# A hybrid decoder layer in fp32: both gate/up and down products of its FFNs in seven block products

## The chip, the cores and the metric

The kernel runs on one core of one Trainium2 chip. The metric is device time in microseconds (us), from the start to the end of one execution; a time given for a kernel is the median of several runs. The core's engines work side by side and wait for each other through semaphores: TensorE (PE in the profile, its weight loads PEld), VectorE (DVE), ScalarE (ACT), GpSimd (POOL) and SyncE (SP). SyncE, ScalarE and GpSimd also start DMA transfers, each on a queue of its own.

## What is computed

The layer has 256 tokens of 2048 channels. Two feed-forward networks (FFNs) with 5632 inner channels stand around a mixer of two attention branches; each of the three steps ends in a LayerNorm.

```
def _swiglu(x, w_gate, w_up, w_down):
    return (jax.nn.silu(x @ w_gate) * (x @ w_up)) @ w_down
...
        h = _layer_norm(ALPHA * h + 0.5 * _swiglu(h, ffn1_w_gate[l], ffn1_w_up[l], ffn1_w_down[l]),
                        ln1_g[l], ln1_b[l])
        mix = _mixer(h, positions, w_in[l], mla_q_norm_g[l], mla_w_uq[l], mla_kv_norm_g[l],
...
        h = _layer_norm(ALPHA * h + mix, ln2_g[l], ln2_b[l])
        h = _layer_norm(ALPHA * h + 0.5 * _swiglu(h, ffn2_w_gate[l], ffn2_w_up[l], ffn2_w_down[l]),
                        ln3_g[l], ln3_b[l])
```

Everything is fp32. The change is in the two FFNs and in how they begin.

## The kernel before

**Products.** TensorE multiplies a 128x128 piece of the activations (held as its stationary operand) by a 128x512 piece of the weights. To keep fp32's accuracy every operand is first split in two: ScalarE rounds it to a short form, `hi` (line 149), and VectorE subtracts that from the original, which gives `lo` (line 150). A product is then three matmuls, hi·hi, hi·lo and lo·hi (`triple`, lines 201 to 204). The tokens stand in two blocks of 128, so a weight piece is used twice, once for each block.

**Weights.** A unit is one DMA of 512 KB: two 128x512 pieces side by side, so 1024 columns. It comes on SyncE's queue into one of four `raw` buffers (or into an `sraw` buffer, see below) and is split into a pair of tiles of the ring `wring`. One unit with both token blocks is worth 12 matmuls. `unit` and `advance` hold a look-ahead: loads are issued some units before the split, and splits some units before the matmuls; `lag` keeps the products of the second token block some units behind those of the first. Buffers bound how early a load can start. Within each engine the build then fixes one order of instructions, and the engine executes in that order: an instruction that waits holds up all behind it.

**Gate/up in seven products.** The 5632 inner channels are worked in 11 pairs of column chunks; a chunk has 256 gate and 256 up columns. The 2048 input channels are four quads of 512, each 2 units of weights. The first pair is computed plainly, with 16 units of 12 matmuls (`project`, called in `ffn`). The pairs 1 to 10 (`Hybrid.group`) treat quads 0 and 1 as a 2x2 block product: quads 0 and 1 of x for the two token blocks against blocks 11, 21 (chunk w0) and 22 (chunk w1) of the weights. Seven block products take the place of eight: products 1 to 7, in two halves of six matmuls each, with sums of x on the one side (the forms `xs`, made once per FFN in `Seven`: sums, differences and a negative, each split) and sums of weight blocks on the other. The sums of weights are made in the buffers themselves: after block 11 has been split for product 1, a DMA from GpSimd adds the corresponding block of w1 to it in place (line 325), and it is split again for product 5; VectorE then joins block 22 to it (line 320), it is split again for 6, and so on. Quads 2 and 3 of x stay plain. Products land in PSUM banks named X, Y, Z, W; ScalarE copies bank X out after products 1, 6 and 7 and Z after 5 (`snap`), and `sum_done` joins bank and copy on VectorE.

**From gate/up to down.** h = silu(gate)·up (lines 503 and 507) is turned on VectorE (line 495) and written to DRAM as `hT` by GpSimd (line 497). `get_h` reads it back by quads (line 525), and `split_h` splits it. Before the down projection the program drains its look-ahead (`look(0, 0)`, `catch_up(0)`, `flush()`). Down takes 11 quads of h against four column chunks, one after the other, 22 units of 12 matmuls each, all plain; h is split in the first chunk and kept for the other three. Each chunk ends in the eviction of two banks into z with its statistics (lines 450 to 454), and after the fourth the LayerNorm is applied block by block (`apply`, lines 459 to 486), transposed by TensorE (line 382) and split for the next stage.

**The beginning.** x is loaded in pieces of 128x512 on ScalarE's queue (line 912, `load_x`) and split as it comes. TensorE runs 32 short matmuls on zeros meanwhile (line 98).

## Time and profile before

| what | value |
| --- | --- |
| median of 3 runs | 2049.41 us (2049.03 to 2052.78) |
| the profiled execution | 2047.69 us, its span from the first to the last instruction 2045.9 us |
| mean granted TensorE clock | 0.996 of full speed |
| DMA | 453.14 MB in all, 221 GB/s over the span |
| joins of gate/up (line 507) | the first at 35.3 us, the last of FFN2 at 1796.4 |
| evictions of down (line 452) | the first at 536.3, the last at 2035.2 us |
| evictions of the mixer into LayerNorm 2 (line 450) | 1268.3 to 1338.6 us |

The span is told in us from its first instruction. FFN1's gate/up goes to about 470 us, its down projection to about 710, the mixer to about 1340, and FFN2 from there to the end. PE, DVE and so on are busy times; a row of the timeline has start, duration, engine, line, operation, output<-inputs, and in square brackets how long the engine had been idle before it and what it waited for.

### The profile page before, as it was taken

To read this page: it belongs to the slowest core of one execution; us is meant where nothing else is said; L and a number is where in the kernel's file an instruction comes from. 1 tells how busy PE (TensorE), PEld (TensorE's weight loads), DVE (VectorE), ACT (ScalarE), POOL (GpSimd) and SP (SyncE) were. 2 spreads that over 40 slices of the span, in tenths; PEclk is the share of its full clock that TensorE was granted. 3 is DMA by queue.
4 is the path that set the end of the run, shared out by engine and by line. 5 is a ranking of instruction groups with operands and counts; after the bars stand their busy time and mean duration, and the time that the engine had idled before them with its cause. 6 is when DMAs were issued, how large, how long until landed. Compare 5 with 4: busy or idle time off the path is not lost.

```text
span 2045.9 us, 25157 instructions
## 1 busy us (share of the span) xinstructions
PE 2019.2 (99%) x9088; PEld 1669.7 (82%) x9088; DVE 1429.5 (70%) x1685; ACT 1146.3 (56%) x1443; POOL 219.9 (11%) x359
## 2 busy tenths in 40 slices
PE   8999999999999999999999999999999999999997
PEld 7788888887888888888888888878888888878886
DVE  6788888887555575455665555688888888865545
ACT  5666666666433565554674445476666666753332
POOL 1112111222000000000000000011211121220000
PEclk9999999999999999999999999999999999999999
DMA  7877887898655756544545575667788788986553
GB/s 274 244 224 225 269 261 224 227 281 318 203 194 194 242 174 202 171 154 153 171 164 187 191 275 187 213 230 233 226 271 258 220 231 271 293 284 195 196 192 138
DMA packets 129437, 453.14 MB, mean 221 GB/s; under 512 B 17104, under 2 KB 17184, under 8 KB 129312
## 3 DMA queue, kind: packets, MB, share of 16 engines
q1 hardware_dynamic: 102240, 366.52, 51.9%
q0 software_dynamic: 25920, 82.91, 17.7%
q10 hardware_dynamic: 1152, 2.10, 0.3%
q8 instruction: 71, 1.16, 0.2%
q14 instruction: 54, 0.44, 0.1%
HBM read 433.64 MB, written 17.83 MB: 221 GB/s over the span
## 4 chain that ended last, share of the span: by engine, by line
PE 87%; DMA 4%; issue 4%; DVE 3%; ACT 1%; POOL 1%; DVEq 0%; ACTq 0%; POOLq 0%; SPq 0%
PE mm L203 28%; PE mm L202 28%; PE mm L204 28%; DVE wring L150 1%; DMA sraw<-in_gu_dram 1%; DMA xraw<-in_xT_dram 1%; DMA hraw<-hT 1%; DMA z<-in_x_dram 1%; ACT wring L149 0%; POOL hT L497 0%; DMA row_i<-in_pos_row_dram 0%; PE tr L382 0%; PE tr L664 0%; DVE h L150 0%; DMA raw<-in_gu_dram 0%
## 5 line engine op out<-in xcount | busy, mean ns | idle before, releaser
L150 DVE TENSOR_TENSOR wring<-raw,wring 128x1024 fp32r<-128x1024 f32 (+1 forms) x582 | 701.9, 1210 | 463.6 <-ACT wring L149 460.2
L149 ACT CAST wring<-raw 128x1024 fp32r<-128x1024 f32 (+1 forms) x582 | 605.0, 1042 | 566.3 <-PE mm L204 507.3
L202 PE MATMUL mm<-wring,h 128*128 128x512 f32 (+2 forms) x1632 | 635.0, 389 | 1.8 <-ACT h L149 1.8
L204 PE MATMUL mm<-wring,h 128*128 128x512 f32 (+2 forms) x1632 | 630.1, 387 | 0.6 <-DVE h L150 0.6
L203 PE MATMUL mm<-wring,h 128*128 128x512 f32 (+2 forms) x1632 | 629.4, 386 | 0.4 <-DVE wring L150 0.4
L149 ACT CAST wring<-sraw 128x1024 fp32r<-128x1024 f32 x280 | 292.6, 1053 | 179.5 <-PE mm L204 74.7
L150 DVE TENSOR_TENSOR wring<-sraw,wring 128x1024 fp32r<-128x1024 f32 x280 | 336.3, 1217 | 51.1 <-ACT wring L149 46.4
L202 PEld LDWEIGHTS mm<-wring,h 128*128 128x128 f32 x1632 | 306.7, 188 | 63.6 <-ACT h L149 3.6
L204 PEld LDWEIGHTS mm<-wring,h 128*128 128x128 f32 x1632 | 306.5, 188 | 63.3 <-DVE h L150 2.2
L203 PEld LDWEIGHTS mm<-wring,h 128*128 128x128 f32 x1632 | 306.7, 188 | 61.5 <-DVE wring L150 1.5
L203 PE MATMUL mm<-wring,xs 128*128 128x512 f32 x560 | 218.8, 391 | 3.9 <-DVE wring L150 3.9
L202 PE MATMUL mm<-wring,xs 128*128 128x512 f32 x560 | 218.4, 390 | 1.6 <-ACT snap L305 1.6
L204 PE MATMUL mm<-wring,xs 128*128 128x512 f32 x560 | 218.4, 390 | 0.0
L202 PE MATMUL mm<-wring,x 128*128 128x512 f32 x384 | 150.6, 394 | 5.7 <-ACT x L149 4.5
L203 PE MATMUL mm<-wring,x 128*128 128x512 f32 x384 | 150.5, 393 | 0.4 <-DVE wring L150 0.4
L204 PE MATMUL mm<-wring,x 128*128 128x512 f32 x384 | 150.0, 392 | 0.0
L203 PEld LDWEIGHTS mm<-wring,xs 128*128 128x128 f32 x560 | 105.4, 188 | 26.7 <-DVE wring L150 5.2
L202 PEld LDWEIGHTS mm<-wring,xs 128*128 128x128 f32 x560 | 105.3, 188 | 24.4 <-ACT snap L305 2.5
L204 PEld LDWEIGHTS mm<-wring,xs 128*128 128x128 f32 x560 | 105.4, 188 | 21.8
L497 POOL DMA_DIRECT2D hT<-blocks x176 | 97.1, 560 | 208.6 <-DVE blocks L495 205.2
L325 POOL DMA_DIRECT2D sraw<-in_gu_dram x80 | 70.4, 880 | 440.5 <-DVE wring L150 380.9
L320 DVE TENSOR_TENSOR sraw<-sraw,sraw 128x1024 f32<-128x1024 f32 x80 | 95.9, 1219 | 0.5
(240 smaller groups left out, 1616.1 us busy)
## 6 DMA issues: line engine op xcount, KB each, us to landing
raw<-in_gu_dram SPq DMA_DIRECT2D x192, 512.0 KB, 5.5
raw<-in_dn_dram SPq DMA_DIRECT2D x176, 512.0 KB, 4.2
sraw<-in_gu_dram SPq DMA_DIRECT2D x120, 512.0 KB, 6.5
sraw<-in_gu_dram POOLq DMA_DIRECT2D x80, 512.0 KB, 8.3
raw<-in_wgm_dram SPq DMA_DIRECT2D x32, 512.0 KB, 3.4
raw<-in_wgd_dram SPq DMA_DIRECT2D x32, 512.0 KB, 3.4
raw<-in_w_out_dram SPq DMA_DIRECT2D x32, 512.0 KB, 3.8
hT<-blocks POOLq DMA_DIRECT2D x176, 64.0 KB, 2.7
```

Of the source, the lines that this page charges most:

```text
L149: S.copy(hi, src)
L150: V.tensor_tensor(out=lo, in0=src, in1=hi.bitcast(F32), op=ALU.subtract)
L202: PE.matmul(o, xh, wh, start=first, stop=False, skip_group_check=again)
L203: PE.matmul(o, xh, wl, start=False, stop=False, skip_group_check=again)
L204: PE.matmul(o, xl, wh, start=False, stop=last, skip_group_check=again)
L320: V.tensor_tensor(out=t, in0=t, in1=R[joins[p]][s], op=ALU.add)
L325: nc.gpsimd.dma_start(R[adds[p]][s], w1[s], accum_op=ALU.add)
L497: nc.gpsimd.dma_start(hT[q, b].rearrange("(g r) (i f) -> i r g f", g=4, i=4)[i], t[32 * i:32 * (i + 1), :].rearrange("r (g f) -> r g f", g=4))
```

## The change

It has four parts.

1. *The first pair of gate/up is in seven products too* (`group` with `opening=True`). Its plain units, quads 2 and 3 of x, come first and the seven products between and behind them; each result has a bank of its own. The forms of x are made by `sevens`, attached to units 5 to 13. PSUM is one pool of eight banks instead of five and three.
2. *x comes on SyncE's queue*, between the weights: quads 2 and 3 first, then 0 and 1, which are not split by themselves any more (only their forms are). LayerNorm 2 hands over in the order 2, 3, 0, 1, for the same reason.
3. *Down is done in two passes of two column chunks each* (`c0`, `c1`). In each pass four of the eleven quads of h (two blocks of two) are in seven products, whose forms are made anew in each pass; seven quads are plain. h is fetched and split in both passes (`get`, `put`, `take`); nothing of it is kept. Product sums are gathered by `gather` into z.
4. *The joints.* Gate/up and down are one list of units; down begins with quads 4 and 5 in its first pass, with 4 in its second, and the look-ahead runs on from the one to the other.

The diff, cut to its core:

```diff
@@ -83,10 +83,10 @@
         return small.tile([P, n], dt, tag="sm", name=nm(name), bufs=24)
 
     def mm_bank(name="mm"):
-        return psum.tile([P, 512], F32, tag="mm", name=nm(name), bufs=5)
+        return psum.tile([P, 512], F32, tag="bank", name=nm(name), bufs=8)
 
     def tr_bank(name="tr"):
-        return psum.tile([P, 512], F32, tag="tr", name=nm(name), bufs=3)
+        return mm_bank(name)
...
+        def sevens(self, d, blocks=False):
+            ra, rc = self.raw(2 * d), self.raw(2 * d + 1)
+            at = self.forms.setdefault(d, {})
+            st = {}
...
+            def sums():
+                a0, a1, c0, c1 = (of_raw(r, b) for r in (ra, rc) for b in range(2))
...
+                for out, in0, in1 in ((f5, a1, c1), (f7, a1, a0), (f6, a0, f5), (f3, c0, f6)):
+                    V.tensor_tensor(out=out, in0=in0, in1=in1, op=ALU.subtract)
...
+            return [minus, lambda: pair(None, 2, 4), sums, lambda: pair(st["a"], 5, 6), lambda: pair(st["b"], 7, 3)]
...
+        def seven(self, d, p, then=None):
+            fresh = {1: ("A", 0, 0), 2: ("E", 0, 2), 3: ("D", 1, 2)}
+            src = {1: "A", 5: "A", 6: "A", 4: "A", 2: "E", 3: "D", 7: "D"}[p]
+            joins = {6: "D", 4: "E"}
+            adds = {1: "A", 6: "D"}
...
+                    t = self.blocks[src, s]
                     if p in joins:
-                        V.tensor_tensor(out=t, in0=t, in1=R[joins[p]][s], op=ALU.add)
+                        V.tensor_tensor(out=t, in0=t, in1=self.blocks[joins[p], s], op=ALU.add)
                     pair = next_pair()
                     split(*pair, t)
                     st["pair"] = [v.rearrange("p (g n) -> p g n", g=G) for v in pair]
                     if p in adds:
-                        nc.gpsimd.dma_start(R[adds[p]][s], w1[s], accum_op=ALU.add)
+                        nc.gpsimd.dma_start(self.blocks[adds[p], s], self.w[1][4 * d + s], accum_op=ALU.add)
...
-            rest = list(range(j0, end))
-            for p, n in ((1, 0), (2, 1), (5, 1), (3, 0), (6, 1), (4, 1), (7, 0)):
...
+        if opening:
+            seq = [(0, 4), (0, 5), (1, 4), (1, 5), (0, 6), 1, (1, 6), 2, (0, 7), 5, (1, 7), 3, 6, 4, 7]
+        else:
+            seq = [1, 2, (0, 4), 5, (0, 5), 3, 6, (0, 6), 4, (0, 7), 7, (1, 4), (1, 5), (1, 6), (1, 7)]
...
-            for c in range(4):
+            for c in (2, 3, 0, 1) if self.x.kept else range(4):
...
-        project(wgu[0], x, KD, 512, lambda b, bank: gu_done(0, b, bank), hook=first_hook)
-        project(wgu[1], x, KD, 512, lambda b, bank: gu_done(1, b, bank), hook=second)
-        look(3, 4)
...
-                later(13, lambda: split_h(0))
...
-        for c in range(4):
-            project(wdn[c], h, KF, 512, lambda b, bank, c=c: ln.evac(c, b, bank), hook=more if c == 0 else dn_hook(c))
...
+        for p in range(KF // 4):
+            items += group(x, wgu[2 * p], wgu[2 * p + 1],
+                           lambda n_, b, bank, snap, op, p=p: sum_done(2 * p + n_, b, bank, snap, op), p == 0)
+        for i, f in zip((5, 7, 10, 11, 13), x.sevens(0)):
+            at(i, f)
+        if first is not None:
+            first(at)
+        at(12, lambda: narrow(), True)
...
+        def get(i, q):
+            nc.gpsimd.dma_start(hx[i].raw(q), hT[q].rearrange("b p f -> p b f"))
...
+        for i, (c0, c1) in enumerate(((0, 1), (2, 3))):
+            pr = Pair(hx[i], wdn[c0], wdn[c1], "stream")
...
+            def seven(d, q, last, i=i, pr=pr, gather=gather):
+                t = len(items)
+                at(t - 16, lambda: get(i, 2 * d))
+                at(t - 14, lambda: get(i, 2 * d + 1))
+                for k, f in enumerate(hx_forms(i, d)):
+                    at(t - 7 + k, f)
+                at(t - 2, lambda: get(i, q))
+                for b in range(2):
+                    at(t + b, lambda b=b: put(i, q, b))
+                pl = [pr.plain(n, 2 * q + g) for n in range(2) for g in range(2)]
+                r = []
+                for p in (1, 2, None, 5, None, 3, 6, None, 4, None, 7):
...
+            if i == 0:
+                at(len(items), lambda: st.update(ln=LayerNorm(0.5, residual, g, bt, each, nxt, cols)), True)
+                for q in (4, 5):
+                    items += lone(q)
+            else:
+                items += lone(4)
+            items += seven(0, 6 if i == 0 else 5, False)
+            items += lone(7 if i == 0 else 6)
+            items += seven(1, 8 if i == 0 else 7, True)
+            if i == 0:
+                for q in (9, 10):
+                    items += lone(q)
+            else:
+                at(len(items) - 8, lambda: st["ln"].take_rows(), True)
+                at(len(items), widen, True)
+                for n in range(2):
+                    for q in (8, 9, 10):
+                        items += lone(q, (n, n), True)
...
     def load_x(q, b):
-        raw = xq.raw(q, b) if q in xq.kept else tmp_tile([P, 512], "xraw")
-        nc.scalar.dma_start(raw, a["xT"][q, b])
-        xq.put(q, b, raw.rearrange("p (k t) -> p k t", k=4))
-
-    def start_hook(j):
-        if j in (2, 4, 6):
-            load_x(j // 2, 0)
-        if 1 <= j < 5:
-            load_x(j - 1, 1)
+        nc.sync.dma_start(xq.raw(q)[:, b, :], a["xT"][q, b])
+        if q > 1:
+            xq.put(q, b, xq.raw(q)[:, b, :].rearrange("p (k t) -> p k t", k=4))
+
+    def first(at):
+        for i, q, b in ((0, 2, 0), (1, 2, 1), (4, 3, 0), (4, 3, 1), (5, 0, 0), (5, 0, 1), (5, 1, 0), (5, 1, 1)):
+            at(i, lambda q=q, b=b: load_x(q, b), True)
```

What this does to the order of the instructions shows at three places. The first is VectorE in FFN1's opening (`raw`, `sraw`: weights as loaded; `wring`: their lo part; `xs`: forms of x). Before, the first block product's weights `sraw_77` are split in the second pair and split again, after the added block, eight rows later:

```order
L150 TENSOR_TENSOR wring_22_125<-sraw_77_451,wring_21_124 128x1024
L150 TENSOR_TENSOR wring_20_123<-sraw_78_452,wring_19_122 128x1024
L150 TENSOR_TENSOR wring_18_121<-sraw_79_453,wring_17_120 128x1024
L150 TENSOR_TENSOR wring_16_119<-sraw_80_454,wring_15_118 128x1024
L507 TENSOR_TENSOR hb_48_285<-mm_55_297,sg_75_442 128x256
L150 TENSOR_TENSOR wring_6_109<-raw_87_468,wring_5_108 128x1024
L150 TENSOR_TENSOR wring_22_125<-sraw_78_452,wring_21_124 128x1024
L507 TENSOR_TENSOR hb_57_312<-mm_63_334,sg_90_494 128x256
L495 STREAM_TRANSPOSE blocks_92_497<-hb_48_285 128x512
L150 TENSOR_TENSOR wring_4_107<-sraw_77_451,wring_3_106 128x1024
```

After, the block is `sraw_40` and stands in the first pair:

```order
L190 TENSOR_TENSOR wring_22_125<-raw_52_306,wring_21_124 128x1024
L190 TENSOR_TENSOR wring_12_115<-sraw_40_229,wring_11_114 128x1024
L190 TENSOR_TENSOR xs_41_234<-neg_42_235,xs_41_234 128x512
L190 TENSOR_TENSOR wring_10_113<-sraw_44_252,wring_9_112 128x1024
L190 TENSOR_TENSOR wring_20_123<-sraw_40_229,wring_19_122 128x1024
L190 TENSOR_TENSOR wring_8_111<-raw_47_266,wring_7_110 128x1024
L190 TENSOR_TENSOR xs_49_271<-xraw_24_128,xs_48_270 128x1024
L190 TENSOR_TENSOR wring_10_113<-sraw_44_252,wring_9_112 128x1024
L190 TENSOR_TENSOR wring_8_111<-raw_58_341,wring_7_110 128x1024
```

The first split has moved forward among the first units, and two rows stand between it and the second.

The second place is TensorE at the end of LayerNorm 2, where FFN2 opens (`h2`: the layer's normalized activations; `tr`: transposes of z; `mm`: banks). Before:

```order
L202 MATMUL mm_1338_9884<-wring_530_4955,h2_1329_9856 128x512
L203 MATMUL mm_1338_9884<-wring_531_4956,h2_1329_9856 128x512
L382 MATMUL tr_1350_9978<-ident_70,z_1251_9273 128x128 x4
L382 MATMUL tr_1353_9992<-ident_70,z_1251_9273 128x128 x4
L382 MATMUL tr_1354_10004<-ident_70,z_1252_9274 128x128 x4
L204 MATMUL mm_1338_9884<-wring_530_4955,h2_1330_9857 128x512
L202 MATMUL mm_1338_9884<-wring_530_4955,h2_1329_9856 128x512
L203 MATMUL mm_1338_9884<-wring_531_4956,h2_1329_9856 128x512
L382 MATMUL tr_1358_10019<-ident_70,z_1252_9274 128x128 x4
L204 MATMUL mm_1338_9884<-wring_530_4955,h2_1330_9857 128x512
L202 MATMUL mm_1365_10041<-wring_524_4949,h2_1351_9987 128x512
```

After:

```order
L246 MATMUL mm_1453_10149<-wring_7_110,h2_1440_10080 128x512
L247 MATMUL mm_1453_10149<-wring_8_111,h2_1440_10080 128x512
L248 MATMUL mm_1453_10149<-wring_7_110,h2_1440_10080 128x512
L430 MATMUL tr_1463_10211<-ident_70,z_1366_9512 128x128 x4
L430 MATMUL tr_1466_10225<-ident_70,z_1366_9512 128x128 x4
L430 MATMUL tr_1469_10239<-ident_70,z_1365_9511 128x128 x4
L430 MATMUL tr_1470_10249<-ident_70,z_1365_9511 128x128 x4
L246 MATMUL mm_1453_10149<-wring_7_110,h2_1440_10080 128x512
L247 MATMUL mm_1453_10149<-wring_8_111,h2_1440_10080 128x512
L248 MATMUL mm_1453_10149<-wring_7_110,h2_1440_10080 128x512
L246 MATMUL mm_1478_10268<-wring_1410_9929,xs_1476_10263 128x512
```

Behind the transposes of the second token block came plain products with `h2`, of this block in a bank of its own; now a block product comes, whose stationary operand is a form `xs`.

The third is VectorE in the down projection. Before, it held splits of weights (`raw`) and evictions into z with their statistics (`bn`):

```order
L150 TENSOR_TENSOR wring_22_125<-raw_481_4359,wring_21_124 128x1024
L150 TENSOR_TENSOR wring_20_123<-raw_483_4378,wring_19_122 128x1024
L452 SCALAR_TENSOR_TENSOR z_379_3535<-mm_458_4005,z_379_3535 128x512
L454 BN_STATS bn_393_3551<-z_379_3535 128x6
L150 TENSOR_TENSOR wring_18_121<-raw_485_4395,wring_17_120 128x1024
L452 SCALAR_TENSOR_TENSOR z_381_3537<-mm_460_4030,z_381_3537 128x512
L454 BN_STATS bn_394_3552<-z_381_3537 128x6
```

After, forms of h (`fa`, `fb`, `xs`), h itself and block A of the weights (`sraw_460`) stand between:

```order
L190 TENSOR_TENSOR wring_22_125<-sraw_460_3666,wring_21_124 128x1024
L168 TENSOR_TENSOR fb_471_3719<-hraw_437_3524,fa_470_3718 128x512
L190 TENSOR_TENSOR xs_474_3742<-fa_470_3718,xs_473_3741 128x1024
L190 TENSOR_TENSOR wring_20_123<-sraw_464_3690,wring_19_122 128x1024
L190 TENSOR_TENSOR xs_477_3763<-fb_471_3719,xs_476_3762 128x1024
L190 TENSOR_TENSOR wring_10_113<-sraw_469_3714,wring_9_112 128x1024
L190 TENSOR_TENSOR wring_8_111<-sraw_472_3736,wring_7_110 128x1024
L190 TENSOR_TENSOR h_480_3812<-hraw_478_3780,h_480_3812 128x512
L190 TENSOR_TENSOR h_483_3826<-hraw_478_3780,h_483_3826 128x512
L190 TENSOR_TENSOR wring_6_109<-raw_475_3757,wring_5_108 128x1024
L190 TENSOR_TENSOR wring_4_107<-sraw_460_3666,wring_3_106 128x1024
L323 TENSOR_TENSOR sraw_460_3666<-sraw_460_3666,sraw_482_3822 128x1024
```

Block A's first split is the first row, its second, after the added block, the last but one; nine rows lie between.

More of the change, by code (lines that the diff above doesn't have):

```diff
@@ L190, in unit @@
             load()
-        loaded.append((prep, now, later_on))
+        todo_now = [*doing, now]
+        doing.clear()
+        loaded.append((prep, lambda: [f() for f in todo_now], later_on))
         advance(*ahead)
@@ L368, in group, with plain @@
[L368 to L377 removed]
+            return [lambda s=s: one(s) for s in range(2)]
+        def plain(self, n, j, then=None, apart=False):
+            return [lambda: self.plain_unit(n, j, then, apart)]
@@ new lines, in plain_unit, with load, prep, products @@
+        def plain_unit(self, n, j, then, apart):
+            st = {}
+            def load():
+                st["raw"] = wpool.tile([P, 1024], F32, tag="raw", name=nm("raw"), bufs=4)
+                nc.sync.dma_start(st["raw"], self.w[n][j])
+            def prep():
+                pair = next_pair()
+                split(*pair, st["raw"])
+                st["pair"] = [v.rearrange("p (g n) -> p g n", g=G) for v in pair]
+            def products(b):
+                wh, wl = st["pair"]
+                o, first = self.bank((n, b))
+                for g in range(G):
+                    k = 2 * j + g
+                    triple(o, self.x.at(0, k, b), self.x.at(1, k, b), wh[:, g, :], wl[:, g, :],
+                           first and g == 0, g == 1, True)
+                if then is not None:
+                    then(b)
+            if apart:
+                unit(load, prep, lambda: products(0), lambda: products(1))
+            else:
+                unit(load, prep, lambda: (products(0), products(1)))
@@ L574, in at_unit @@
+        for i, item in enumerate(items):
+            for f in before.get(i, ()):
+                f()
+            doing.extend(attached.get(i, ()))
+            item()
     def at_unit(u, fn):
```

361 lines of the change are left out of this document (195 added, 166 removed).

## The prediction

> **What bounds the kernel now.** I read the summary of the page first, then the busy time of the engines in stretches that follow the stages, then the groups of instructions.
>
> ```profile
> span 2045.9 us, 25157 instructions
> PE 2019.2 (99%) x9088; PEld 1669.7 (82%) x9088; DVE 1429.5 (70%) x1685; ACT 1146.3 (56%) x1443; POOL 219.9 (11%) x359
> ```
>
> TensorE is busy for 99% of the span, so the time is the number of matmuls times their pitch, plus a few stalls. The table by stretches (columns: length, then busy time and count of PE, PEld, DVE, ACT, POOL; granted clock, DMA share, GB/s) shows where they are.
>
> ```profile
> 0.00:50.00 50.00, 44.10 (x186) 36.39 (x187) 33.11 (x39) 28.54 (x36) 5.49 (x16) 0.93 0.78 271
> 50.00:100.00 50.00, 45.16 (x189) 36.06 (x188) 38.94 (x60) 29.94 (x37) 9.90 (x16) 0.97 0.85 247
> 100.00:430.00 330.00, 330.00 (x1457) 273.29 (x1457) 286.94 (x301) 210.41 (x245) 64.33 (x97) 1.00 0.83 244
> 430.00:520.00 90.00, 87.44 (x382) 70.97 (x381) 69.41 (x79) 58.25 (x74) 26.72 (x48) 1.00 0.87 289
> 520.00:710.00 190.00, 190.00 (x840) 157.39 (x839) 97.84 (x87) 77.84 (x74) 0.54 (x1) 1.00 0.63 204
> 1330.00:1400.00 70.00, 69.18 (x315) 55.51 (x315) 60.93 (x86) 48.19 (x79) 12.35 (x20) 1.00 0.67 214
> 1790.00:1860.00 70.00, 68.53 (x301) 55.69 (x300) 46.72 (x53) 35.85 (x45) 14.06 (x26) 1.00 0.76 261
> 2020.00:2046.00 26.00, 15.12 (x67) 12.20 (x65) 15.02 (x32) 0.41 (x2) 0.00 (x0) 0.89 0.22 81
> ```
>
> From 100 to 430 us (gate/up in seven products) 330 us hold 1457 matmuls, 0.2265 us each, with no gap; VectorE is busy for 87% of it. In the down projection (520 to 710) VectorE has only 51%. The first 100 us hold 375 matmuls, 32 of them short warming ones; the other 343 are worth 77.7 us, so TensorE is 22.3 us late by then. The joints from gate/up to down lose 2.6 and 1.5 us.
>
> What the splits cost is in the groups (mean ns after the comma):
>
> ```profile
> L150 DVE TENSOR_TENSOR wring<-raw,wring 128x1024 fp32r<-128x1024 f32 (+1 forms) x582 | 701.9, 1210 | 463.6 <-ACT wring L149 460.2
> L149 ACT CAST wring<-raw 128x1024 fp32r<-128x1024 f32 (+1 forms) x582 | 605.0, 1042 | 566.3 <-PE mm L204 507.3
> L320 DVE TENSOR_TENSOR sraw<-sraw,sraw 128x1024 f32<-128x1024 f32 x80 | 95.9, 1219 | 0.5
> L612 DVE SCALAR_TENSOR_TENSOR bias<-dist,mask 128x384 f32<-128x384 f32 x4 | 2.0, 551 | 0.0
> L630 DVE SCALAR_TENSOR_TENSOR ang<-turns,ang 128x128 f32<-128x128 f32 x12 | 3.4, 280 | 0.0
> ```
>
> Back to back they overlap a little, as the timeline shows:
>
> ```profile
> 5.51 0.69 DVE L150 TENSOR_TENSOR x<-xraw,x 128x512 fp32r<-128x512 f32 x1 [4.51 <-ACT x L149]
> 18.08 1.90 DVE L150 TENSOR_TENSOR x<-xraw,x 128x512 fp32r<-128x512 f32 x3 [0.35 <-ACT x L149]
> 22.24 4.73 DVE L150 TENSOR_TENSOR wring<-raw,wring 128x1024 fp32r<-128x1024 f32 x4
> 435.16 0.43 DVE L507 TENSOR_TENSOR hb<-gus,sg 128x256 f32<-128x256 f32 x1 [0.61 <-ACT sg L503]
> ```
>
> Four of 1024 columns take 4.73 us, a pitch of 1.17; three of 512 take 1.90, a pitch of 0.61; one of 256 costs some 0.36.
>
> **The change, part by part.**
>
> *Fewer matmuls: -27.2 us.* An opening pair of gate/up goes from 16 x 12 = 192 products to 7 x 12 + 8 x 12 = 180. A down pass (two of the four column chunks) goes from 44 x 12 = 528 to 504, as each of its two blocks saves 12. Per FFN that is 12 + 48 = 60, in all 120 x 0.2265 = 27.2. The Trainium skill (TensorE: Matmul & The Clock Gate, "Wait - 56ns, not 53.3ns?") gives 215.7 ns for a warm pitch of 512 columns; by it this term would be 25.9 us, but here 1457 matmuls show 226.5 ns, and the row decides.
>
> *The joints: -4.0 (0 to -4.1).* Before, everything is drained and h is then fetched and split. After, down begins with quads 4 and 5, written several groups earlier, and leaves 9 and 10 to the end. The 2.6 + 1.5 us go; next late is VectorE.
>
> *Down on VectorE: +4 (0 to +22).* Per FFN the change makes of 88 splits 112, and adds 16 joins, a second splitting of h and the forms of its four blocks: 128 x 1.17 = 149.8; 28 pieces of h x 0.61 = 17.1; forms 4 x (7 x 0.61 + 2 x 1.17) = 26.4; bank sums, joins into z, evictions and statistics 32 x 0.61 = 19.5; the tail of the last gate/up group 5.1. That is 218 us against 1008 x 0.2265 = 228.3: VectorE goes from 51% to 95%, with 10 us to spare. Into that falls a wait: block A is split, w1 is added to it by a DMA from GpSimd, and it is split again.
>
> ```profile
> L325 POOL DMA_DIRECT2D sraw<-in_gu_dram x80 | 70.4, 880 | 440.5 <-DVE wring L150 380.9
> sraw<-in_gu_dram POOLq DMA_DIRECT2D x80, 512.0 KB, 8.3
> ```
>
> Issue 0.9, landing 8.3 and ScalarE's cast 1.05 make 10.2 us; in the order of the changed program VectorE has 9 operations (8.9 us) in between, so some 1.4 us per block and 5.6 per FFN would be lost if all the spare time were used. It mostly isn't: I take 2 per FFN. The upper end is a wait of 4 us in each of four blocks (a landing of 11 us) with half of the spare usable: 11 per FFN. Everything behind the waiting split on VectorE's queue, weights and evictions, is then late too, and TensorE waits for those.
>
> *FFN1's opening: +4 (-5 to +17).* What goes is the wait for x:
>
> ```profile
> 17.06 1.22 PE L202 MATMUL mm<-wring,x 128*128 128x512 f32 x2 [4.45 <-ACT x L149]
> 18.08 1.05 PE L203 MATMUL mm<-wring,x 128*128 128x512 f32 x2
> 87.72 0.80 PE L203 MATMUL mm<-wring,xs 128*128 128x512 f32 x1 [3.18 <-DVE wring L150]
> 15.00:20.00 5.00, 2.94 (x7) 2.36 (x8) 2.61 (x5) 3.61 (x8) 0.00 (x0) 0.60 0.75 289
> 20.00:25.00 5.00, 5.00 (x17) 3.96 (x17) 5.00 (x6) 3.96 (x6) 0.00 (x0) 0.72 0.44 121
> 85.00:90.00 5.00, 2.28 (x5) 1.82 (x6) 5.00 (x12) 2.74 (x3) 0.00 (x0) 0.77 0.84 299
> ```
>
> After the 4.45 us the granted clock was 0.60 and 0.72: 24 matmuls took 7.94 us busy instead of 5.4, 2.5 us more. After the 3.18 us it was 0.77 and five matmuls took 2.28 instead of 1.13. So I put some 2 us of slow clock behind each new stall of over 3 us. The Trainium skill (TensorE: Matmul & The Clock Gate, "Part 1: The HAM clock gate") lets the clock fall to half after about one idle window of 3.4 us and rise after one busy window; an estimate by that page is 1.7 us lost behind each long stall, a cost that speaks against a change that makes new ones. By that rule, the trace roughly agrees, except that 3.18 us of waiting was enough. The first work now needs only quads 2 and 3 of x. But the opening loads VectorE: 26 wide operations 30.4, x 4 x 0.61 = 2.4, forms 6.6, sums and evictions 6.3, together 45.7 us where TensorE has 40.8 (before: 33 against 43.5). The second group adds 35.5 and the setup some 8 (L612 and L630 are 5.4 of it). VectorE starts at 5.5, so after two groups (360 matmuls, 81.5 us) TensorE is 5.5 + 89.2 - 81.5 = 13.2 us late plus VectorE's waits. Those I put at 13: 4 for quad 3 and block A, which stand on SyncE's queue behind weights that wait for a buffer, 8 for the added block, which VectorE wants back after only two operations (1.8 us against 10.2), 1 for others. 26.2 against 22.3 is +4. With 4 us of waits it is -5, with 26 (VectorE idled 27.9 in the first 100 us before) +17.
>
> *FFN2's opening: +11 (+3 to +18).* Before, the second token block's LayerNorm was hidden:
>
> ```profile
> 1338.58 0.68 DVE L450 TENSOR_TENSOR z<-mm,z 128x512 f32<-128x512 f32 x1
> 1347.34 1.91 DVE L478 TENSOR_SCALAR z<-z,mv,f 128x512 f32<-128x512 f32 x4
> 1351.08 0.69 DVE L150 TENSOR_TENSOR h<-h2raw,h 128x512 fp32r<-128x512 f32 x1
> 1341.57 0.26 DVE L460 BATCH_NORM_AGGREGATE mv<-bn 128x2 f32<-128x24 f32 x1
> 1345.94 0.22 DVE L405 SCALAR_TENSOR_TENSOR t<-y,w 128x1 f32<-128x1 f32 x1
> 1348.04 1.47 PE L382 MATMUL tr<-ident,z 128*128 128x128 f32 x12
> ```
>
> From the eviction to the first split of block 1 went 13.2 us, covered by 46 matmuls and 16 transposes (10.4 + 1.9): that window (1330 to 1400, above) lost 0.8 us in all. After, TensorE has 33 matmuls and the transposes (9.4 us) before the first seven-product, whose weights and form VectorE splits behind the whole LayerNorm: 17 wide operations x 0.61, the four of L478 in 1.91, six small ones in some 0.7, 1.17 + 0.61: 14.8 us. The stall is 5.4, the low clock behind it about 2, and the added block, again wanted back after three wide operations (10.2 - 3.0), leaves 4 that nothing covers. The low end is half of the stall alone, the high end adds a second wait in the next group.
>
> *LayerNorm 1 into the mixer: +1 (0 to 3)*, since VectorE comes to it without a lead. The gate/up groups themselves and the 10.9 us tail behind the last matmul keep their instructions: 0.
>
> Sum: -27.2 - 4.0 + 4 + 4 + 11 + 1 = -11.2. The profiled execution took 2047.69 us (span 2045.9 and 1.8 around it), 1.7 under the median of 2049.41. So I forecast 2049.4 - 11.2 = **2038**, with 2028 to 2045 as this case's own range.
>
> **Rivals.** The measurement tells about 0.2%, 4 us, from no change.
>
> 1. *VectorE becomes the bound in the down passes* (slower). Place: the second split of block A in each of eight blocks. Price: the term is +22 instead of +4, so 2056. It decides once the waits use up the 10 us of spare per FFN and 8 more. For it: 95% load and a strict order; against it: the gate/up groups run at 87% without a gap. Chance 0.22.
> 2. *The openings cost 12 us more* because the waits behind the adding DMA come twice: 2050, no change. For it, the landing time of the added block within the first 50 us, where it is 9.3 instead of the 8.3 over the whole run:
>
> ```profile
> sraw<-in_gu_dram POOLq DMA_DIRECT2D x1, 512.0 KB, 9.3
> ```
>
> Against it: TensorE has products of other units in the queue. Chance 0.19.
> 3. *The openings are covered* (-5 and +3) and down costs nothing: -27.2 - 4 - 5 + 3 + 0 + 1 = -32, cut to 2025 as not all come together. For it: the lost 4.45 us and the slow clock go for sure; against it: VectorE's sums. Chance 0.14.
>
> That products are not saved is excluded by the order of the program. The forecast keeps 0.45. Faster by over 0.2%: 0.45 + 0.14 less 0.02 from the forecast's upper edge, 0.57; within 0.2%: 0.20; slower: 0.23. The range reaches from 2021 to 2058: it leaves out the lower part of rival 3 and the upper of rival 1, and with them the ends at which every term is at its worst.
>
> **What would show it.** Right: about 2988 512-column products in each FFN at 0.2265 us; DVE at 90 to 97% in the down passes and PE idle under 3 us there; stalls of TensorE on DVE wring or xs of 4 to 8 us soon after LayerNorm 2; no wait on x over 2 us in the first 25 us; DVE near 100% from 25 to 110 us. Wrong: PE idle over 8 us in a down pass (rival 1), or an opening of FFN2 without a stall (rival 3).

## The result, and the profile after

The changed kernel takes 2126.06 us (median of 4 runs, 2124.58 to 2128.8) beside 2049.97 of the kernel before on the same chip: a ratio of 1.037, 95% interval 1.0352 to 1.0388. It is 76 us slower, where 11 us faster was forecast, and lies far above the range that ended at 2058. The profiled execution took 2124.58 us, with this span and these busy times:

```profile
span 2122.7 us, 25232 instructions
PE 2032.3 (96%) x8968; PEld 1659.4 (78%) x8968; DVE 1611.9 (76%) x1905; ACT 1231.5 (58%) x1569; POOL 262.2 (12%) x399
```

TensorE has 120 instructions fewer, as counted, and is still busy for longer: 96% of a longer span. Busy time also holds the matmuls at a slow clock, so the count in a stretch says more. The table by stretches, of the changed kernel (length, then busy time and count of PE, PEld, DVE, ACT, POOL; granted clock, DMA share, GB/s):

```profile
0.00:50.00 50.00, 39.78 (x149) 30.11 (x150) 24.23 (x28) 22.00 (x27) 6.60 (x17) 0.86 0.79 256
50.00:100.00 50.00, 37.51 (x141) 28.19 (x141) 41.08 (x51) 28.02 (x35) 11.19 (x17) 0.89 0.71 195
150.00:450.00 300.00, 296.88 (x1299) 242.75 (x1298) 253.69 (x259) 183.47 (x216) 55.11 (x84) 1.00 0.83 243
490.00:700.00 210.00, 202.53 (x872) 165.19 (x871) 181.33 (x195) 132.26 (x156) 30.72 (x42) 0.98 0.86 277
1400.00:1450.00 50.00, 44.49 (x177) 34.74 (x175) 39.80 (x42) 31.97 (x37) 3.37 (x4) 0.93 0.71 203
1450.00:1500.00 50.00, 45.27 (x188) 36.07 (x189) 40.99 (x44) 25.59 (x30) 12.27 (x20) 0.97 0.72 206
```

Before, the first 100 us held 375 matmuls; now 290. The stretch from 490 to 700 us, most of it down projection, where VectorE was to be the bound, has 872 (919 before), and VectorE is busy for only 86% of it: it waits as well. To place the loss I took the starts of the last join of each gate/up part (`hb`) and the last eviction of each of the three stages that end in a LayerNorm, from the timelines of VectorE. These are the changed kernel's:

```profile
515.98 0.42 DVE L567 TENSOR_TENSOR hb<-gus,sg 128x256 f32<-128x256 f32 x1
758.17 0.69 DVE L512 SCALAR_TENSOR_TENSOR z<-mm,z 128x512 f32<-128x512 f32 x1
1379.73 0.68 DVE L510 TENSOR_TENSOR z<-mm,z 128x512 f32<-128x512 f32 x1
1871.35 0.42 DVE L567 TENSOR_TENSOR hb<-gus,sg 128x256 f32<-128x256 f32 x1
2111.70 0.69 DVE L512 SCALAR_TENSOR_TENSOR z<-mm,z 128x512 f32<-128x512 f32 x1 [0.39 <-PE mm L248]
```

The kernel before had the same marks at 479.04, 720.83, 1338.58, 1796.38 and 2035.16. So the stages took, in us:

| stage | before | after | products saved | lost |
| --- | --- | --- | --- | --- |
| FFN1 gate/up | 479.0 | 516.0 | 2.7 | 39.7 |
| FFN1 down | 241.8 | 242.2 | 10.9 | 11.3 |
| mixer, to LayerNorm 2 | 617.7 | 621.6 | 0 | 3.8 |
| FFN2 gate/up | 457.8 | 491.6 | 2.7 | 36.5 |
| FFN2 down | 238.8 | 240.3 | 10.9 | 12.4 |

27.2 us were saved and 103.7 lost. Both gate/up parts lose most of theirs in the opening, and both downs give back what they save.

**What TensorE waits for in the opening.** One of its waits behind 100 us, and the wait of ScalarE behind which it stands:

```profile
108.47 0.50 PE L246 MATMUL mm<-wring,xs 128*128 128x512 f32 x1 [2.05 <-ACT wring L189]
```

```profile
103.63 1.05 ACT L189 CAST wring<-sraw 128x1024 fp32r<-128x1024 f32 x1 [7.36 <-DMA sraw<-in_gu_dram]
```

A block of weights came late; by the order of the program it is `sraw_84` of the second pair, and the addition to it, which GpSimd issued at 93.4 us. Such additions the kernel before has in its second pair too. (TensorE's longest wait near it, 3.4 us up to 99.2, stands behind VectorE's wait for `invf`, a small table of the mixer.) The loads of blocks come late as well. SyncE's queue shows this (the changed kernel's timeline of SP; a row of several has the time from the first to the end of the last):

```profile
44.43 0.33 SPq L351 DMA_DIRECT2D raw<-in_gu_dram  x1
44.80 4.76 SPq L318 DMA_DIRECT2D sraw<-in_gu_dram  x8
81.17 6.19 SPq L351 DMA_DIRECT2D raw<-in_gu_dram  x2
87.41 3.02 SPq L318 DMA_DIRECT2D sraw<-in_gu_dram  x5
```

Nothing is issued from 49.6 to 81.2 us; then two plain loads, and behind them five block loads. The waits of that queue in the first 110 us, of the changed kernel and of the one before:

```profile
SPq L351 <- DVE wring L190: 89.9, 11, 31.6
```

```profile
SPq L346 <- DVE wring L150: 27.7, 9, 8.9
SPq L227 <- DVE wring L150: 19.7, 11, 6.7
SPq L346 <- DVE ang L631: 10.3, 1, 10.3
```

A plain load waits until the split that empties its `raw` buffer (there are four) is done. That by itself harms nothing: its weights are wanted later. But the queue issues in order, and the block loads behind it, whose buffers are free (their own waits in these 110 us make 1.1 us) and whose weights are wanted sooner, wait too. The order of the program shows how the loads stand (SyncE, changed kernel): `raw_67`, `raw_80`, `raw_104` and `raw_106` are split only after the blocks `sraw_50` to `sraw_60`, and stand ahead of most of them. (The gap up to 81.2 us comes from the same order one buffer round later: the next plain load waits until `raw_67` has been split.)

```
L318 DMA sraw_40_229<-in_gu1_dram 128x1024
L351 DMA raw_67_438<-in_gu1_dram 128x1024
L351 DMA raw_80_490<-in_gu1_dram 128x1024
L318 DMA sraw_44_252<-in_gu1_dram 128x1024
L318 DMA sraw_50_280<-in_gu1_dram 128x1024
L351 DMA raw_104_628<-in_gu1_dram 128x1024
L318 DMA sraw_51_296<-in_gu1_dram 128x1024
L351 DMA raw_106_666<-in_gu1_dram 128x1024
L318 DMA sraw_59_343<-in_gu1_dram 128x1024
L318 DMA sraw_60_345<-in_gu1_dram 128x1024
```

### The profile page after: what moved, and what is told of

It reads as the page before. It is cut to its first block, busy times and chain, and to the rows that moved or that the text cites. A ratio compares the mean times of both kernels' runs of the same rounds, so it can differ in the third digit from the quotient of the medians.

```text
span 2122.7 us, 25232 instructions
## 1 busy us (share of the span) xinstructions
PE 2032.3 (96%) x8968; PEld 1659.4 (78%) x8968; DVE 1611.9 (76%) x1905; ACT 1231.5 (58%) x1569; POOL 262.2 (12%) x399
## 4 chain that ended last, share of the span: by engine, by line
PE 57%; DMA 13%; DVE 11%; issue 9%; ACT 4%; POOL 1%; ACTq 0%; DVEq 0%; SPq 0%; POOLq 0%
PE mm L246 18%; PE mm L248 18%; PE mm L247 18%; DVE wring L190 6%; DMA sraw<-in_gu_dram 5%; DMA hraw<-hT 3%; ACT wring L189 2%; DMA raw<-in_dn_dram 2%; DMA sraw<-in_dn_dram 1%; DVE sraw L323 1%; DMA z<-res 1%; DMA lv<-in_lam_dram 1%; POOL sraw L328 1%; DVE h L190 1%; DMA z<-in_x_dram 0%
## 5 line engine op out<-in xcount | busy, mean ns | idle before, releaser
L190 DVE TENSOR_TENSOR wring<-raw,wring 128x1024 fp32r<-128x1024 f32 (+2 forms) x502 | 601.1, 1205 | 283.3 <-ACT wring L189 282.6
L189 ACT CAST wring<-raw 128x1024 fp32r<-128x1024 f32 (+2 forms) x502 | 515.7, 1038 | 360.0 <-PE mm L248 287.4
L189 ACT CAST wring<-sraw 128x1024 fp32r<-128x1024 f32 x420 | 436.0, 1050 | 295.4 <-DVE sraw L323 101.7
L190 DVE TENSOR_TENSOR wring<-sraw,wring 128x1024 fp32r<-128x1024 f32 x420 | 504.3, 1218 | 102.2 <-ACT wring L189 100.4
L246 PE MATMUL mm<-wring,h 128*128 128x512 f32 (+2 forms) x1344 | 528.1, 393 | 13.3 <-ACT snap L392 5.5
L247 PE MATMUL mm<-wring,h 128*128 128x512 f32 (+2 forms) x1344 | 522.4, 389 | 3.6 <-DVE wring L190 3.5
L248 PE MATMUL mm<-wring,h 128*128 128x512 f32 (+2 forms) x1344 | 521.6, 388 | 0.7 <-DVE h L190 0.4
L246 PE MATMUL mm<-wring,xs 128*128 128x512 f32 x840 | 333.9, 398 | 25.9 <-ACT wring L189 13.8
L247 PE MATMUL mm<-wring,xs 128*128 128x512 f32 x840 | 335.1, 399 | 17.4 <-DVE wring L190 17.3
L248 PE MATMUL mm<-wring,xs 128*128 128x512 f32 x840 | 331.4, 395 | 1.6 <-DVE xs L190 1.5
L246 PEld LDWEIGHTS mm<-wring,h 128*128 128x128 f32 x1344 | 254.6, 189 | 68.1 <-ACT snap L392 7.9
L247 PEld LDWEIGHTS mm<-wring,h 128*128 128x128 f32 x1344 | 254.9, 190 | 56.3 <-DVE wring L190 7.1
L248 PEld LDWEIGHTS mm<-wring,h 128*128 128x128 f32 x1344 | 254.6, 189 | 53.7 <-DVE h L190 2.6
L246 PEld LDWEIGHTS mm<-wring,xs 128*128 128x128 f32 x840 | 160.3, 191 | 66.9 <-ACT wring L189 19.2
L247 PEld LDWEIGHTS mm<-wring,xs 128*128 128x128 f32 x840 | 160.8, 191 | 60.5 <-DVE wring L190 27.1
L248 PEld LDWEIGHTS mm<-wring,xs 128*128 128x128 f32 x840 | 160.6, 191 | 35.0 <-DVE xs L190 2.3
L246 PE MATMUL mm<-wring,x 128*128 128x512 f32 x352 | 139.5, 399 | 10.9 <-ACT snap L392 5.7
L323 DVE TENSOR_TENSOR sraw<-sraw,sraw 128x1024 f32<-128x1024 f32 x120 | 144.0, 1220 | 1.3 <-DMA sraw<-in_gu_dram 0.3
L247 PE MATMUL mm<-wring,x 128*128 128x512 f32 x352 | 139.2, 396 | 2.0 <-DVE wring L190 2.0
L248 PE MATMUL mm<-wring,x 128*128 128x512 f32 x352 | 138.9, 395 | 0.0
```

Of the source, the lines that this page charges most:

```text
L189: S.copy(hi, src)
L190: V.tensor_tensor(out=lo, in0=src, in1=hi.bitcast(F32), op=ALU.subtract)
L246: PE.matmul(o, xh, wh, start=first, stop=False, skip_group_check=again)
L247: PE.matmul(o, xh, wl, start=False, stop=False, skip_group_check=again)
L248: PE.matmul(o, xl, wh, start=False, stop=last, skip_group_check=again)
L323: V.tensor_tensor(out=t, in0=t, in1=self.blocks[joins[p], s], op=ALU.add)
```

## The experiments

My first theory (A) was another: that the splits wait for the blocks that GpSimd's DMA adds to, and in down for pieces of h caught between such DMAs. The rival B was VectorE's load. Theory S, the order of SyncE's queue, came only after the first four runs. Times are medians; ratios are to the kernel before on the same chip.

**1. A plain opening.** Both first pairs in 16 plain units; the changes that go with it (all of x is split, its pieces come a little earlier) are left out here.

```diff
-        for p in range(KF // 4):
+        pr0 = Pair(x, wgu[0], wgu[1], "open")
+        for m in range(2):
+            for j in (4, 5, 6, 7, 0, 1, 2, 3):
...
+                items += pr0.plain(m, j, e0, True)
+        for p in range(1, KF // 4):
```

> The first pair of gate/up is plain again in both FFNs (16 units of 12 products; all of x is split), x still comes on SyncE's queue, down stays as changed. Theory A (the loss is waiting for transfers on GpSimd's queue: the added blocks in the openings, the pieces of h in down): the joins of pair 1 stood 28.6 us (FFN1) and 22.9 us (FFN2) later than before, all of it goes: 2126 - 51 = 2075 us. Rival X (x on the weights' queue is what costs in FFN1): only FFN2's 23 us go, 2103. Rival B (VectorE's load is the loss): down keeps its 24 us and the opening gives back at most its surplus on VectorE, some 10 us each, 2106.

2086.39 us (1.0183, 1.0167 to 1.0198): 40 us back, less than A's 51, more than X and B said. FFN1's gate/up ended at 497.1 instead of 516.0 us, FFN2's took 470.8 instead of 491.6. The opening is the larger part; something in the rest of the FFNs is left.

**2. No added blocks in the opening.**

```diff
-                    if p in adds:
+                    if p in adds and self.kind != "open":
```

> As the changed kernel, but in the first pair of each FFN the eight DMAs that add w1 to a block are left out, so that pair's weights are wrong; all splits, joins and products stay. Theory A: the splits wait for the block no longer; in the trace of the changed kernel TensorE lost some 20 us in FFN1's first 111 us and some 13 us in FFN2's opening behind such splits, so 2126 - 25 to 33 = 2093 to 2101. Rival B (VectorE's load): the same number of VectorE operations, so within 8 us of 2126.

2132.78 us (1.0404, 1.0389 to 1.042): nothing saved; the time is 7 us higher, and why is not known. Theory A alone does not explain the loss of the openings, and ScalarE's waits in the first 110 to 120 us say why, of the changed kernel and of this run:

```profile
ACT wring L189 <- DMA sraw<-in_gu_dram: 21.3, 7, 7.4
```

```profile
ACT wring L189 <- DMA sraw<-in_gu_dram: 20.9, 7, 6.5
```

The row does not tell a load of a block from an addition to it; both write `sraw`. The order of the program does: of the 21.3 us, 4.2 are for an addition of the opening, 11.0 for additions of the second pair, which this run keeps, and 6.1 for loads. In this run the 4.2 are gone, and a load made up for them, that of `sraw_51`, which SyncE's queue issued at 44.6 us, right behind a plain load that had waited:

```profile
49.16 1.05 ACT L189 CAST wring<-sraw 128x1024 fp32r<-128x1024 f32 x1 [5.31 <-DMA sraw<-in_gu_dram]
```

**3. Early pieces of h.**

```diff
-                at(t - 2, lambda: get(i, q))
+                at(t - 12, lambda: get(i, q))
```

> As the changed kernel, but in down the piece of h that is plain within a seven-product block is fetched 12 units ahead instead of 2, so that it stands on GpSimd's queue before the adding DMAs and not between them. Theory A: the waits of ScalarE for h (5 to 6 us, some four of them, TensorE loses 3 to 5 us behind each) go: 2126 - 10 to 16 = 2110 to 2116. Rival B (VectorE at 95% in down): the load stays, within 4 us of 2126.

2133.06 us (1.0402, 1.0387 to 1.0418): no gain; the downs take 242.7 and 240.7 us, about as before this edit (242.2 and 240.3). The waits that it removes are real. GpSimd's queue and ScalarE in the changed kernel:

```profile
676.74 0.84 POOL L328 DMA_DIRECT2D sraw<-in_dn_dram  x1 [21.32 <-DVE wring L190]
677.28 1.04 POOL L598 DMA_DIRECT2D hraw<-hT  x1
```

```profile
686.12 1.14 ACT L189 CAST h<-hraw 128x512 fp32r<-128x512 f32 x2 [5.89 <-DMA hraw<-hT]
```

The fetch of h stands behind an adding DMA that waited 21 us for VectorE's split, and h lands 9 us after. But with that wait gone others took its place, and B seemed to hold. It did not, as run 11 and the stretch of run 14 further below show.

**4. All of down plain** (still two passes, h streamed twice).

```diff
-            items += seven(0, 6 if i == 0 else 5, False)
-            items += lone(7 if i == 0 else 6)
-            items += seven(1, 8 if i == 0 else 7, True)
+            for q in ((0, 1, 2, 3, 6, 7, 8) if i == 0 else (0, 1, 2, 3, 5, 6, 7)):
+                items += lone(q)
```

> As the changed kernel, but all eleven quads of h are plain in both passes of down (h is still fetched and split twice, the list still runs on from gate/up). 96 products more than the changed kernel (+21.7 us). Theory A: the 24 us that the two down projections lose against the count of products go with the blocks, and 4 to 7 us at each joint may go too: 2126 + 22 - 24 to 35 = 2113 to 2124. Rival J (the running-on of the list and the second fetching cost, not the blocks): the loss stays, 2126 + 22 = 2148.

2120.31 us (1.0339, 1.0322 to 1.0356), with 96 products more. The downs took 239.2 and 236.9 us, which is their 1056 products at 0.2265: streaming h twice costs nothing, and the loss comes with the blocks. J falls; the time lies where A put it, without showing which of the blocks' waits it is.

**5. Loads in the order of use.** Each load of weights in an FFN gets a dependence on the load before it that fixes the order of issue and makes nothing wait.

```diff
+        if last_load:
+            tc.add_manual_dep(ins.ins, last_load[0].name, mybir.DependencyInfo(
+                mybir.DependencyClass.NoSync, mybir.DependencyReason.DATA), reason="load order")
+        last_load[:] = [ins.ins]
...
-                    nc.sync.dma_start(t, self.w[n0][4 * d + o + s])
+                    ordered(nc.sync.dma_start(t, self.w[n0][4 * d + o + s]), self)
```

> As the changed kernel, but the loads of weights of both FFNs stand on SyncE's queue in the order in which they are used; in the changed kernel loads into the four raw buffers stand ahead of block loads that are used earlier, and while such a load waits for its buffer (89.9 us of waiting in the first 110 us, 31.6 the longest) the block loads behind it are not issued. Theory S (this queue order is the loss of the openings): FFN1's opening gets back 15 to 20 us, FFN2's 8 to 13, the other groups of gate/up some 4 each: 2126 - 31 to 41 = 2085 to 2095. Rival B (VectorE's load): within 8 us of 2126. Rival A (the adding DMAs) has lost its run already, where leaving them out saved nothing; by it, too, nothing changes here.

2090.96 us (1.0194, 1.0176 to 1.0212): 35 us back with every instruction kept (the build then also places a few splits of plain weights elsewhere on VectorE and ScalarE). Theory S holds. FFN1's gate/up is 16.8 us shorter and FFN2's 13.3, though SyncE's queue still waits for 63.1 of the first 110 us: what counts is what stands behind the wait. It reaches past the openings: from 150 to 450 us, the ordinary groups, there are 27 matmuls (6 us) more.

```profile
150.00:450.00 300.00, 300.00 (x1326) 248.48 (x1325) 256.69 (x265) 189.15 (x221) 56.80 (x86) 1.00 0.83 249
```

**6, 7 and 8. Ordered loads, with a plain down, without the added blocks of the opening, and with a plain opening.** The edits are those of runs 4, 2 and 1 on top of run 5.

> Loads in the order of use, and all quads of h plain in down (96 products, 21.7 us, more). Theory S with a down that has no slack on VectorE: down with blocks loses what it saves, so this is 0 to 6 us under the run with ordered loads and blocks. Rival D (down's loss, too, is the order of loads): the blocks then save their 21.7 us in the other run, and this one is 15 to 22 us above it.

2097.7 us (1.0222, 1.0207 to 1.0237): 6.7 above run 5, so the blocks in down now earn 7 of their 21.7 us. D is right in part.

> Loads in the order of use, and the adding DMAs of the first pair of each FFN left out (its weights are wrong by that). Theory S alone: within 4 us of the run with ordered loads. Theory S with A behind it (once the loads come in time, the splits wait for the added blocks): 8 to 16 us under it.

2085.53 us (1.0162, 1.0147 to 1.0177): 5.4 under run 5, between the two: with the loads in time the added blocks cost a little, 4.3 of it in FFN1's gate/up (494.9 us instead of 499.2).

> Loads in the order of use, and the first pair plain in both FFNs. Theory S: the stalls that the run with the plain opening still had behind late loads (7.4 us at 81.5 us) and some 4 us per FFN in the groups go: 2086 - 10 to 18 = 2068 to 2076; and an opening in seven products that is not held up by loads is within 5 us of it or under it. Rival O (the opening in seven products is too dense for VectorE whatever the loads do): this run stays 15 us or more under the one with ordered loads alone.

2058.86 us (1.0035, 1.0023 to 1.0047): better than expected, and 32 us under run 5. Rival O's condition came true; whether VectorE is the reason was the next question.

**9. Less work for VectorE in the opening.** On top of run 5; the low parts of the weights of five products are not computed in the first pair.

```diff
-                    split(*pair, t)
+                    if self.kind == "open" and p in (5, 3, 6, 4, 7):
+                        S.copy(pair[0], t)
+                    else:
+                        split(*pair, t)
```

> Loads in the order of use, opening in seven products, but in the first pair of each FFN the low parts of the weights of products 5, 3, 6, 4 and 7 are not computed (VectorE's ten wide subtractions per opening are left out, so the values are wrong). Rival O (VectorE is what holds the opening once the loads come in time): 10 x 1.14 = 11.4 us less work per opening, 15 to 23 us in all: 2091 - 15 to 23 = 2068 to 2076. Theory S alone (only waits for loads are left): within 5 us of 2091.

2083.88 us (1.017, 1.0155 to 1.0185): 7 us, less than O said and more than S, some 4 of them in FFN1's gate/up and none in FFN2's (495.5 and 478.3 us, run 5: 499.2 and 478.3). VectorE is not what holds FFN2's opening.

**10 and 11. The joint, and h early again.** On top of run 8. Run 10 scales the residual z 12 units later (`later(4, ...)` to `later(16, ...)` for FFNs). Run 11 adds the edit of run 3 and fetches the other pieces 16 units ahead instead of 11.

> Ordered loads, plain opening, and ScalarE's scaling of the residual z at the joint 12 units later. Theory J (at each joint ScalarE waits 4 to 5 us for z, which GpSimd's queue fetches 11 us before, and the copy of a bank behind it holds TensorE 4.0 and 5.5 us): 2059 - 6 to 9 = 2050 to 2053. Rival (the copy is held by the pieces of h or the weights instead): within 3 us of 2059.

2063.04 us (1.0063, 1.0046 to 1.008): nothing gained. But the run hardly tested it: the build kept the first scaling of z where it was, 12.3 us behind the fetch at the second joint (11.5 in run 8), where ScalarE waited 5.3 us for it (4.5 in run 8). Only the last two of the four scalings moved.

> As the run before, and every piece of h is fetched earlier: 12 units ahead instead of 2 within a block, 16 instead of 11 for the others. If the waits for h (5.5 us of ScalarE, 1 to 2.5 us of TensorE at some three places in each down) are what down still loses: 4 to 10 us under the run before. If VectorE's load is: within 3 us of it.

2047.4 us (0.9986, 0.9974 to 0.9998). Early fetches, which gained nothing in run 3, gain 16 us with the loads in order (and with the other pieces early too, which run 3 did not have): the downs took 229.0 and 227.2 us, the count of their products. The reading that fits is that two queues each held the same engines, and freeing one left the other; the share of the other pieces was not tried alone. The joints still lost 5 to 6 us: TensorE waited 5.1 and 5.9 us there for ScalarE's copy of a bank. At the second one, ScalarE and the transfers that were then under way:

```profile
1777.77 1.06 ACT L497 ACTIVATE z<-z 128x1024 f32<-128x1024 f32 x1 [5.05 <-DMA z<-res]
```

```profile
hraw<-hT POOLq DMA_DIRECT2D x4, 512.0 KB, 12.0
z<-res POOLq DMA_DIRECT2D x4, 512.0 KB, 13.6
```

**12 and 13. The residual's fetch itself later, and x on ScalarE's queue.** Run 12 is run 11 without run 10's edit and with the LayerNorm, which fetches z, made 25 units after the joint; run 13 puts x back on ScalarE's queue.

```diff
-                at(len(items), lambda: st.update(ln=LayerNorm(0.5, residual, g, bt, each, nxt, cols)), True)
+                at(len(items) + 25, lambda: st.update(ln=LayerNorm(0.5, residual, g, bt, each, nxt, cols)), True)
```

> Ordered loads, plain opening, early pieces of h, and the LayerNorm's residual z (2 MB on GpSimd's queue) fetched 25 units later instead of at the joint. Theory Z (the joint's 5.2 and 6.1 us are that fetch: it fills the transfer engines just when h is wanted, and ScalarE waits 5 us for z with the copy of a bank behind it): 2047 - 8 to 11 = 2036 to 2039. Rival (the joint is held by the pieces of h or the weights, z or not): within 3 us of 2047.

> As the run before, but x comes on ScalarE's queue again, in the same order of pieces. If x on the weights' queue helps or harms by more than the stalls that are left in the first 30 us (some 5 us in all), this differs by 3 us or more; otherwise within 3 us.

2035.66 us (0.9927, 0.9911 to 0.9944) and 2032.99 us (0.9915, 0.9901 to 0.9929): both beat the kernel before. Theory Z holds for the joints. As the fetch and the scaling of z moved together, it stays open which of the two, the full transfer engines or ScalarE's wait, held them. The last 50 us of each gate/up part, of run 11 and then of run 12, show the joints gone:

```profile
430.00:480.00 50.00, 44.92 (x192) 36.69 (x191) 38.01 (x41) 31.81 (x38) 11.29 (x18) 0.97 0.86 275
1746.00:1796.00 50.00, 44.08 (x185) 35.95 (x183) 37.28 (x39) 31.30 (x38) 11.32 (x18) 0.93 0.85 264
```

```profile
430.00:480.00 50.00, 50.00 (x222) 41.44 (x221) 43.03 (x48) 31.87 (x40) 9.10 (x14) 1.00 0.87 263
1746.00:1796.00 50.00, 49.70 (x220) 40.82 (x219) 42.63 (x47) 31.28 (x39) 9.20 (x15) 1.00 0.85 259
```

At FFN1 the gain did not last, in the profiled executions at least: run 12's gate/up was 6.9 us shorter, and its down 7.6 us longer (236.6 us instead of 229.0), with a wait of 3.6 us for a split of h and slow matmuls behind it near its end. The spans differ by 5.2 us, the medians by 11.7.

x on ScalarE's queue is 2.7 us faster, and the intervals overlap: what that part of the change does is too small to tell.

**14 and 15. The price of the openings alone.** Run 12 with the first pair in seven products again, in both FFNs (14) and in FFN1 only (15).

> The changed kernel with its first pair in seven products in both FFNs, but with ordered loads, early pieces of h and the residual fetched later: beside the run with the residual fetched later (2036) it prices the openings alone. By the stages of the earlier runs (gate/up and hand-over 14.7 and 13.9 + 5.8 us longer): 2036 + 30 to 36 = 2066 to 2072. If the openings' cost was an effect of the late pieces and the joints: under 2050.

> As the run before, but only FFN1 opens in seven products; FFN2's first pair is plain. Theory H (FFN2's cost is the hand-over from LayerNorm 2, whose second token block no product of another kind covers any more: TensorE did 37 matmuls in 20 us there; FFN1's cost is apart from it): 2036 + 13 to 17 = 2049 to 2053. If FFN1's opening costs all of it: 2066 or more; if FFN2's does: under 2040.

2070.23 us (1.0106, 1.0089 to 1.0122) and 2049.43 us (0.9995, 0.9984 to 1.0006): 13.8 us for FFN1's opening and 20.8 for FFN2's, though they have 24 products (5.4 us) fewer. FFN1's is the less certain: its gate/up took 17.2 us longer in run 15 than in run 12, and part of that is hidden because run 12 lost time in down, as above. The first 20 us behind LayerNorm 2's last eviction, of the kernel before, of the changed one, and of runs 12 and 14:

```profile
1338.60:1358.60 20.00, 19.97 (x95) 15.88 (x94) 19.93 (x39) 15.78 (x37) 3.81 (x7) 1.00 0.51 177
```

```profile
1379.70:1399.70 20.00, 13.23 (x57) 10.35 (x56) 15.88 (x31) 12.13 (x31) 5.78 (x10) 0.83 0.46 153
```

```profile
1338.70:1358.70 20.00, 20.00 (x94) 15.76 (x93) 19.48 (x38) 15.77 (x38) 4.34 (x8) 1.00 0.54 180
```

```profile
1354.90:1374.90 20.00, 9.20 (x34) 6.99 (x35) 14.58 (x26) 10.88 (x25) 3.92 (x6) 0.74 0.76 237
```

With 16 transposes among them, run 14 has 18 products there and the plain openings 78 or 79. In run 14 TensorE waits first for the second token block's z and then for the first form, which is made behind it:

```profile
1358.34 2.09 PE L441 MATMUL tr<-ident,z 128*128 128x128 f32 x16 [3.46 <-DVE z L549]
1367.78 0.80 PE L246 MATMUL mm<-wring,xs 128*128 128x512 f32 x1 [7.35 <-ACT xs L189]
```

FFN1's opening loses more between 20 and 40 us than in any other 20. The kernel before, run 14, and run 7, which leaves the additions out:

```profile
20.00:40.00 20.00, 20.00 (x83) 16.18 (x83) 16.64 (x18) 14.16 (x17) 0.00 (x0) 0.93 0.61 202
```

```profile
20.00:40.00 20.00, 13.91 (x49) 10.47 (x48) 10.71 (x11) 9.35 (x11) 1.76 (x2) 0.83 1.04 361
```

```profile
20.00:40.00 20.00, 17.24 (x74) 13.25 (x73) 16.28 (x17) 12.43 (x16) 0.00 (x0) 1.00 0.93 360
```

In run 14 the transfer engines are full (a share of 1.04, 361 GB/s) and nobody else is: the opening wants 18 units of 512 KB in the time of 180 products where the plain one wants 16 in that of 192, beside x. The stall is ScalarE's wait for the first block with an addition, behind which TensorE waited 6.1 us. GpSimd issued that addition at 21.6 us; run 7, without it and with the transfer engines nearly as full, has no such wait:

```profile
30.96 1.04 ACT L189 CAST wring<-sraw 128x1024 fp32r<-128x1024 f32 x1 [9.50 <-DMA sraw<-in_gu_dram]
```

The Trainium skill (DMA: Bandwidth & Descriptors, "Where 436 GB/s comes from") puts the limit between HBM and SBUF at about 358 GB/s per core. The trace does not show it as a limit: from 10 to 20 us the same run moved 399 GB/s.

These 20 us are not the whole price. From 40 to 140 us run 12, with a plain opening, and run 14 compare so:

```profile
40.00:140.00 100.00, 94.44 (x404) 76.40 (x404) 87.37 (x117) 65.06 (x79) 17.66 (x27) 0.98 0.78 241
```

```profile
40.00:140.00 100.00, 85.79 (x341) 66.95 (x340) 85.15 (x117) 59.06 (x73) 19.15 (x29) 0.94 0.61 167
```

There 63 more matmuls are missing, at a DMA share of 0.61. So full transfer engines explain only a part.

## Why the prediction failed, step by step

*Fewer matmuls, -27.2:* right; TensorE has 120 instructions fewer, and in run 11 the downs take the time of their products.

*FFN1's opening, +4.* This is the step that failed first, in the sentence "Those I put at 13": the waits. It named SyncE's queue ("4 for quad 3 and block A, which stand on SyncE's queue behind weights that wait for a buffer") but took one such wait, where the queue waited for 89.9 us in the first 110 with block loads behind it. FFN1's gate/up lost 39.7 us, and putting the loads in order alone gave 16.8 of them back (run 5). The sum's other part, that VectorE's work bounds the opening, did not come true either: it was to be near 100% busy from 25 to 110 us and was at 82% from 50 to 100. The added block, to which I gave 8 us, held ScalarE for 4.2 us in the changed kernel; leaving it out gained nothing while a load was late in its place (run 2), and some 4 us with the loads in order (run 7). The price that stayed when the loads were in order, 16.5 us with the 2.7 of saved products, is near the upper end of the range that I gave (+17). VectorE's low parts explain some 4 us of it (run 9); the transfers of the first 40 us have a part in it, whose size no run shows.

*FFN2's opening, +11:* the stall that I worked out is there, and larger: 5.4 us and 2 of slow clock were forecast; beside the kernel before, the 20 us behind LayerNorm 2 lack 38 products, 8.6 us, in the changed kernel (41 products and 16 transposes of 57) and 61, 13.8 us, in run 14. The mechanism was right and its size too small; behind it came the queue of SyncE again, which I had not priced here at all: the order of loads gave FFN2's gate/up 13.3 us back (run 5).

*Down on VectorE, +4 (0 to +22):* 11.3 and 12.4 us were lost, just over the upper end, but not by VectorE's load. Run 14 has the same blocks and the same instructions of VectorE, whose load is higher as nothing waits:

```profile
490.00:700.00 210.00, 208.83 (x921) 172.28 (x920) 195.14 (x210) 141.51 (x165) 35.17 (x49) 1.00 0.88 286
```

VectorE at 93% holds up TensorE for 1.2 of 210 us. Rival 1 gave the right price for the wrong reason. The block's added weights were my reason for it; the fetch of h behind that adding DMA on GpSimd's queue was what I overlooked, with the order of the program at hand to show it; beside it stood SyncE's queue again, whose order cost 6.6 and 3.7 us of the two downs (run 5).

*The joints, -4.0:* they did not go. The drained look-ahead went, and the next late thing, which I took to be VectorE, was the residual of 2 MB that the LayerNorm fetches at that moment (runs 11 and 12).

*LayerNorm 1 into the mixer, +1:* the stretch to LayerNorm 2 lost 3.8 us; why was not tried.

Rival 2 (openings 12 us dearer) had the right place, but the two gate/up parts were 61 us dearer (39.7 and 36.5 against 4 and 11), and its reason, the adding DMA, explains 5.4 us (run 7). That rival 1's price fitted was luck. In ratios, the way back from 1.037 is: loads in order to 1.0194, h early and the residual late to 1.0106, plain openings to 0.9927. What stays open: why the build puts the loads in that order, why runs 2 and 3 came out 7 us slower than the changed kernel, and how the 13.8 us of FFN1's opening divide between transfers, VectorE and the added blocks.

## What to carry to other kernels

A queue that issues in order is a shared resource like an engine: for every load, ask what stands ahead of it and what that waits for, and read it from the order of the program, because a load whose buffer is not free stops all loads behind it. When an edit that removes a visible wait gains nothing, a second queue may hold the same engines; try it again after the other is freed before blaming the load of the engine that waits, and see in the order of the program that the edit moved what it was to move. A change may save work in one place and pay in another: here blocks in down are worth their 21.7 us once fed (run 11), blocks in an opening, where nothing covers the waits, are not.
